# Modulation ahead of h: three of eight k-blocks of the adaLN product go from VectorE to TensorE

## The chip, the cores and the metric

The kernel runs on one core of one Trainium2 chip. The metric is the device time of one execution in microseconds (us), and lower is better. The engines are called as in the profile: PE is TensorE (PEld is its weight loads), DVE is VectorE, ACT is ScalarE, POOL is GpSimd, SP is SyncE, which issues the DMAs here.

## The reference, cut to what matters

One layer of a decoder trunk reads a normalized input `h` that is modulated by a vector `c`. Everything behind it (two token mixers, their merge, an output projection and a last norm) starts from `h`:

```python
ada = jax.nn.silu(c) @ w_ada + b_ada
shift, scale, gate = jnp.split(ada, 3, axis=-1)
h = _rmsnorm(x, norm_w) * (1.0 + scale[:, None, :]) + shift[:, None, :]
proj = jnp.einsum("bsd,de->bse", h, w_in)
...
```

`x` is 1024 tokens by 1024 channels in float32, `c` is one row of 1024, `w_ada` is 1024 by 3072, and `w_in` is 1024 by 8472. The change concerns the first line alone, for `shift` and `scale`: a product of one row by a matrix.

## The kernel before

All channels are cut into eight blocks of 128, numbered by `k` where they are the channels of `h`. The front of the kernel, its first 80 us or so, does the following.

SP loads `x` in eight tiles `xt` (128 tokens each), the part of `w_ada` for shift and scale in eight tiles `wa` of 1 MB (one for each `k`, five buffers), and the first weights of `w_in` (`wr`). Each `xt` is squared and summed on ACT (L259), its factor is made on POOL (`rs`, L262), and DVE scales it in place (L263).

`ada_cols(k)` makes shift and scale for the 128 channels of block `k`. Tile `was[k]` holds, on 128 partitions, eight k-blocks of the sum over the input channels, each with 256 columns (128 for scale, 128 for shift). DVE multiplies each of the eight blocks with its column of `cols` (silu of `c`) and adds them up in `acc`, 128x256: one instruction at L287 and seven at L289. What is left is the sum over the 128 partitions, and TensorE does it with two matmuls (L291) whose weights are the halves of `acc` and whose moving operand is a single column of ones. They write two columns of the bank `cp`, of which there is one buffer. DVE reads them into the columns `av` (L294) and `sv` (L296).

`h_half(k, hf)` makes block `k` of `h` for one half of the tokens. TensorE transposes four pieces of `xt` into the bank `tp` (L302), ACT applies `av` and `sv` (`xa`, L305) and rounds to the high part `hh` (L306), and DVE subtracts to get the low part `hl` (L307). Float32 products are made from three matmuls on high and low parts.

`c_half` (L115 to L117) multiplies: for three slabs of `w_in` at a time (`FIRST`), nine matmuls with 512 moving columns for each block `k` and token half, accumulated over all `k` in the banks `mm` (first half) and `um` (second half). So these products follow `h` block by block.

Behind the front, DVE and POOL form sums of the blocks of `h` (`pe`, L440 to L444) for a product scheme with fewer multiplications, and TensorE goes on with the other projections.

The order of the instructions on each engine isn't that of the code. A scheduler in the compiler sorts the whole program along a timeline of its own before it is built, and each engine then works through its list strictly in that order.

Of the kernel before, what the change touches and what calls it, by code (L numbers as in the profile page):

```python
# [31 lines left out]
P = 128  # L32
# [32 lines left out]
PAIRS += [(G0 + 12, G0 + 13), (G0 + 14, G0 + 15)]  # L65
R_C, R_SHIFT, R_SCALE, R_NW, R_SNW, R_BG, R_CB, R_CW = 0, 8, 16, 24, 32, 40, 56, 66
NROWS = 106


def build(ctx, tc, t):  # L70
    nc = tc.nc
    V, A, G, PE, SP = nc.vector, nc.scalar, nc.gpsimd, nc.tensor, nc.sync
# [75 lines left out]
    ones = const.tile([P, P], F32, name="ones")  # L148
# [5 lines left out]
    V.memset(mhalf, -0.5)  # L154
    cols = const.tile([P, NROWS], F32, name="cols")
    hb = const.tile([P, 40], F32, name="hb")
# [45 lines left out]
    with tc.tile_pool(name="st", bufs=1, side="right") as st, \  # L202
            tc.tile_pool(name="stp", bufs=1, space=PSUM) as stp:
        vrow = st.tile([NROWS, P], F32, name="vrow")
        SP.dma_start(out=vrow, in_=t["vecs"])
        xts, was, uraw = {}, {}, {}
# [31 lines left out]
        vps = stp.tile([P, 512], F32, tag="tp", bufs=1, name="tp")  # L238
        PE.transpose(out=vps[:, :NROWS], in_=vrow, identity=ident[:NROWS, :NROWS])
        V.tensor_copy(out=cols, in_=vps[:, :NROWS])  # L240
        V.tensor_scalar(out=cols[:, R_CB:NROWS], in0=cols[:, R_CB:NROWS], scalar1=0.5, scalar2=None, op0=ALU.mult)
        V.tensor_scalar(out=cols[:, R_BG:R_BG + 16], in0=cols[:, R_BG:R_BG + 16], scalar1=0.5, scalar2=None,
# [37 lines left out]
        def ada_cols(k):  # L280

            cp = stp.tile([P, 512], F32, tag="cp", bufs=1, name="cp")
            acc = st.tile([P, 256], F32, tag="acc", bufs=2, name="acc")
            for kk in range(8):
                w = was[k][:, kk, :]
                if kk == 0:
                    V.tensor_scalar(out=acc, in0=w, scalar1=cols[:, kk:kk + 1], scalar2=None, op0=ALU.mult)  # L287
                else:
                    V.scalar_tensor_tensor(out=acc, in0=w, scalar=cols[:, kk:kk + 1], in1=acc, op0=ALU.mult, op1=ALU.add)  # L289
            for i in range(2):  # L290
                PE.matmul(cp[:, 2 * i:2 * i + 1], lhsT=acc[:, i * P:(i + 1) * P], rhs=ones[:, 0:1],  # L291
                          start=True, stop=True)
            a, sh = av[:, k:k + 1], sv[:, k:k + 1]
            V.scalar_tensor_tensor(out=a, in0=cp[:, 0:1], scalar=cols[:, R_SCALE + k:R_SCALE + k + 1],  # L294
                                   in1=cols[:, R_NW + k:R_NW + k + 1], op0=ALU.add, op1=ALU.mult)
            V.tensor_tensor(out=sh, in0=cp[:, 2:3], in1=cols[:, R_SHIFT + k:R_SHIFT + k + 1], op=ALU.add)  # L296
# [12 lines left out]
        for k in range(2):  # L309
            ada_cols(k)  # L310
            h_half(k, 0)
        for k in range(2):
            h_half(k, 1)
        for k in range(2, 8):
            ada_cols(k)
            for hf in range(2):
                h_half(k, hf)
# [312 lines left out]
    with tc.tile_pool(name="sd", bufs=1, side="right") as sd, \  # L630
# [152 lines left out]
        for tb in range(8):  # L783
            PE.matmul(rps[:, 2 * tb:2 * tb + 1], lhsT=sacc[:, tb * P:(tb + 1) * P], rhs=ones[:, 0:1],
                      start=True, stop=True)
# [455 lines left out]
```

## Time and profile before

| | |
|---|---|
| median of 3 runs | 1285.14 us (1281.14 to 1290.57) |
| the profiled execution | 1286.09 us, of which the span of its instructions is 1284.4 us |
| busy share of the span | PE 92%, PEld 77%, DVE 75%, POOL 60%, ACT 46% |
| mean granted clock of TensorE | 0.974 |

A busy share is an average over the whole span. The front has other limits than the rest, so the views below are cut to stretches of it.

### The profile page before, as it was taken

What the parts mean: (1) busy time and instruction counts of PE and PEld (TensorE: products, weight loads), DVE (VectorE), ACT (ScalarE), POOL (GpSimd) and SP (SyncE); (2) the same over time, 40 slices, a digit from 0 to 9 for tenths busy, and PEclk for the clock granted to TensorE, in tenths of its full rate; (3) what the DMA queues carried; (4) which work ended last, traced back from release to release, by engine and by line L of the source; (5) the groups of instructions that cost most, each with busy time, mean ns of one, the idle gap of its engine ahead of it and who ended that gap; (6) DMA issues with size and microseconds to landing.
All of it is one profiled execution on the core that took longest, in us unless ns stands there. A gap on an engine that the chain in (4) does not pass through costs nothing. (4 is left out here: it accounts for less than half of the span.)

```text
span 1284.4 us, 18783 instructions
## 1 busy us (share of the span) xinstructions
PE 1183.9 (92%) x6206; PEld 988.8 (77%) x6206; DVE 963.1 (75%) x1618; ACT 594.8 (46%) x1194; POOL 776.1 (60%) x644
## 2 busy tenths in 40 slices
PE   4897899999978999999988999999999999999896
PEld 3686688777766788799778888888887787878685
DVE  6979767787799566348689764545667968999997
ACT  5443324242423232477667733444456553444354
POOL 3258465474755476448887966435446635587666
PEclk9998899998989999999999999999999999999999
DMA  8422443624556566654565558623236619766143
GB/s 346 158 100 98 160 123 124 213 64 167 188 185 216 175 211 228 223 177 148 188 200 163 173 191 296 210 87 116 74 127 210 201 55 328 224 188 193 52 116 145
DMA packets 104126, 219.70 MB, mean 171 GB/s; under 512 B 11818, under 2 KB 19420, under 8 KB 103004
## 3 DMA queue, kind: packets, MB, share of 16 engines
q1 hardware_dynamic: 104028, 218.50, 51.5%
q8 instruction: 49, 0.80, 0.3%
q14 instruction: 49, 0.40, 0.1%
HBM read 154.85 MB, written 63.61 MB: 170 GB/s over the span
## 5 line engine op out<-in xcount | busy, mean ns | idle before, releaser
L103 POOL TENSOR_TENSOR wl<-wr,wh 128x512 fp32r<-128x512 f32 (+1 forms) x188 | 281.5, 1508 | 135.7 <-ACT wh L102 130.7
L102 ACT CAST wh<-wr 128x512 fp32r<-128x512 f32 (+1 forms) x214 | 129.8, 618 | 158.4 <-DMA wr<-w_c 53.7
L103 POOL TENSOR_TENSOR sl<-sr,sh 128x512 fp32r<-128x512 f32 x57 | 91.0, 1603 | 78.8 <-ACT sh L102 65.7
L115 PE MATMUL mm<-hh,wh 128*128 128x512 f32 x288 | 115.9, 407 | 4.3 <-ACT wh L102 1.9
L116 PE MATMUL mm<-hl,wh 128*128 128x512 f32 x288 | 116.7, 405 | 3.0 <-DVE hl L307 3.0
L117 PE MATMUL mm<-hh,wl 128*128 128x512 f32 x288 | 116.3, 405 | 0.0
L102 ACT CAST sh<-sr 128x512 fp32r<-128x512 f32 x57 | 34.1, 619 | 96.6 <-DVE sr L478 77.0
L140 PE MATMUL mm<-wh,hh 128*128 128x256 f32 (+1 forms) x256 | 74.9, 294 | 3.8 <-DVE tmp L348 3.8
L141 PE MATMUL mm<-wl,hh 128*128 128x256 f32 (+1 forms) x256 | 74.8, 293 | 0.0
L142 PE MATMUL mm<-wh,hl 128*128 128x256 f32 (+1 forms) x256 | 74.4, 292 | 0.0
L1018 ACT ACTIVATE pr<-pr,sm 128x1024 f32<-128x1024 f32 (+3 forms) x64 | 49.9, 780 | 50.4 <-DVE sm L1017 42.4
L1021 POOL TENSOR_SCALAR pr<-pr,sm 128x1024 f32<-128x1024 f32 (+3 forms) x64 | 48.6, 762 | 34.7 <-DVE sm L1020 30.2
L1013 DVE CUSTOM_DVE_ANT_0 pr<-lg,fb 128x512 f32<-128x512 f32 (+1 forms) x96 | 51.5, 551 | 23.5 <-PE lg L1012 14.0
L115 PEld LDWEIGHTS mm<-hh,wh 128*128 128x128 f32 x288 | 55.1, 193 | 15.6 <-ACT wh L102 2.4
L116 PEld LDWEIGHTS mm<-hl,wh 128*128 128x128 f32 x288 | 55.3, 192 | 14.7 <-DVE hl L307 3.9
L1004 POOL TENSOR_SCALAR_AFFINE_SELECT fb<-fb 128x128 f32<-128x128 f32 x64 | 21.9, 344 | 72.1 <-DVE sm L1013 57.3
L117 PEld LDWEIGHTS mm<-hh,wl 128*128 128x128 f32 x288 | 55.2, 192 | 10.8
L1037 DVE TENSOR_TENSOR ptl<-tp,pth 128x512 fp32r<-128x512 f32 (+1 forms) x80 | 50.1, 632 | 15.9 <-ACT pth L1036 15.5
L1036 ACT CAST pth<-tp 128x512 fp32r<-128x512 f32 (+1 forms) x80 | 42.3, 543 | 41.5 <-PE tp L1033 32.4
L683 ACT ACTIVATE ab<-ab,acs 128x128 f32<-128x128 f32 x128 | 41.1, 391 | 31.7 <-DMA ab<-a_scr 28.1
L140 PEld LDWEIGHTS mm<-wh,hh 128*128 128x128 f32 x256 | 49.5, 194 | 4.7 <-DVE tmp L348 4.5
L103 POOL TENSOR_TENSOR m<-ab,m 128x512 fp32r<-128x512 f32 x32 | 46.7, 1462 | 7.1 <-ACT m L102 4.7
(393 smaller groups left out, 3972.6 us busy)
## 6 DMA issues: line engine op xcount, KB each, us to landing
wr<-w_c SPq DMA_DIRECT2D x116, 256.0 KB, 3.5
wa<-w_ada SPq DMA_DIRECT2D x8, 1024.0 KB, 11.4
g_scr<-gt SPq DMA_DIRECT2D x16, 512.0 KB, 4.0
ab<-a_scr SPq DMA_DIRECT2D x32, 256.0 KB, 3.7
gt<-g_scr SPq DMA_DIRECT2D x32, 256.0 KB, 3.0
wr<-w_ps SPq DMA_DIRECT2D x28, 256.0 KB, 2.9
wr<-w_pa SPq DMA_DIRECT2D x28, 256.0 KB, 3.1
wr<-so SPq DMA_DIRECT2D x28, 256.0 KB, 2.6
```

The source lines that it names most:

```text
L102: A.copy(out=hi[:, :n], in_=raw[:, :n])
L103: eng.tensor_tensor(out=lo[:, :n], in0=raw[:, :n], in1=f32(hi[:, :n]), op=ALU.subtract)
L115: PE.matmul(ps, lhsT=hi[:, cs], rhs=xh[k][:, hs], start=(k == 0), stop=False)
L116: PE.matmul(ps, lhsT=hi[:, cs], rhs=xl[k][:, hs], start=False, stop=False)
L117: PE.matmul(ps, lhsT=lo[:, cs], rhs=xh[k][:, hs], start=False, stop=(k == 7))
L140: PE.matmul(o, lhsT=xh[k][:, ts], rhs=hi[:, cs], start=(k == 0), stop=False)
L141: PE.matmul(o, lhsT=xh[k][:, ts], rhs=lo[:, cs], start=False, stop=False)
L142: PE.matmul(o, lhsT=xl[k][:, ts], rhs=hi[:, cs], start=False, stop=(k == 7))
L1013: V.tensor_tensor_reduce(out=pr[:, n0:n1], in0=lg[:, :n1 - n0], in1=fb[:, n0:n1], op0=ALU.add, op1=ALU.min, scale=1.0, scalar=BIG, accum_o ...
L1018: A.activation(out=pr[:, :n], in_=pr[:, :n], func=AF.Exp, scale=-1.0, bias=sm[:, 0:1], accum_out=sm[:, 1:2])
L1021: G.tensor_scalar(out=pr[:, :n], in0=pr[:, :n], scalar1=sm[:, 1:2], scalar2=0.5, op0=ALU.mult, op1=ALU.mult)
L1037: V.tensor_tensor(out=ptl[:, :w], in0=tp[:, :w], in1=f32(pth[:, :w]), op=ALU.subtract)
```

## The change

A constant `NV = 5` is added. DVE sums up the first five k-blocks only. The other three go to TensorE as matmuls of their own, with a 128x128 piece of `was[k]` as weights and the column of `cols` as the moving operand, into the same column of `cp` into which the sum of `acc` then goes, with `acc` last. The type of all of them is float32, as it was for `acc`.

```diff
+NV = 5
...
-            for kk in range(8):
+            for kk in range(NV):
                 w = was[k][:, kk, :]
...
             for i in range(2):
-                PE.matmul(cp[:, 2 * i:2 * i + 1], lhsT=acc[:, i * P:(i + 1) * P], rhs=ones[:, 0:1],
-                          start=True, stop=True)
+                o = cp[:, 2 * i:2 * i + 1]
+                for kk in range(NV, 8):
+                    PE.matmul(o, lhsT=was[k][:, kk, i * P:(i + 1) * P], rhs=cols[:, kk:kk + 1], start=(kk == NV),
+                              stop=False)
+                PE.matmul(o, lhsT=acc[:, i * P:(i + 1) * P], rhs=ones[:, 0:1], start=False, stop=True)
```

For all eight `k` together these are 24 instructions less on DVE (three of the seven at L289, eight times) and 48 matmuls more on TensorE (three for each of two columns, eight times). Four lines are added in the code, so L291 becomes L296 (the new matmuls are L294), L302 becomes L306, and c_half's L115 to L117 become L116 to L118.

The scheduler makes another order of it within the front. From DVE's last `hl` on, the instructions of all five engines stand in the same order as before.

On TensorE, around the products of block `k` = 3 (`hh_234` and `hl_242`; `hh_235` is block 4), before:

```order
L291 MATMUL cp<-ones,acc 128x1 x2
L116 MATMUL um<-hl_242,wh 128x512
L117 MATMUL um<-hh_234,wl 128x512
L116 MATMUL um<-hl_242,wh 128x512
L117 MATMUL um<-hh_234,wl 128x512
L116 MATMUL um<-hl_242,e_379 128x512
L117 MATMUL um<-hh_234,e_379 128x512
L291 MATMUL cp<-ones,acc 128x1 x2
L302 MATMUL tp<-ident,xt 128x128 x4
L115 MATMUL mm<-hh_235,wh 128x512 x2
```

and the same place after:

```order
L118 MATMUL um<-hh_234,e_379 128x512
L294 MATMUL cp<-cols,wa 128x1 x3
L296 MATMUL cp<-ones,acc 128x1
L294 MATMUL cp<-cols,wa 128x1 x3
L306 MATMUL tp<-ident,xt 128x128 x4
L296 MATMUL cp<-ones,acc 128x1
L116 MATMUL mm<-hh_235,wh 128x512
L117 MATMUL mm<-hl_243,wh 128x512
L118 MATMUL mm<-hh_235,wl 128x512
```

Eight one-column matmuls of one `k` now stand between two groups of nine c_half matmuls, where two stood. The group shown of after is that of `k` = 7, the last one. The two shown of before are those of `k` = 4 and 5; those of `k` = 6 and 7 came later, one behind each half of the products of block 5.

On VectorE, from the start of the sum for `k` = 4 (DVE's row L287) on, before:

```order
L287 TENSOR_SCALAR acc<-wa,cols 128x256
L289 SCALAR_TENSOR_TENSOR acc<-wa,cols,acc 128x256 x4
L307 TENSOR_TENSOR hl_241<-xa,hh_233 128x512
L289 SCALAR_TENSOR_TENSOR acc<-wa,cols,acc 128x256
L294 SCALAR_TENSOR_TENSOR av<-cp,cols 128x1
L296 TENSOR_TENSOR sv<-cp,cols 128x1
L287 TENSOR_SCALAR acc<-wa,cols 128x256
L289 SCALAR_TENSOR_TENSOR acc<-wa,cols,acc 128x256 x2
L307 TENSOR_TENSOR hl_241<-xa,hh_233 128x512
L289 SCALAR_TENSOR_TENSOR acc<-wa,cols,acc 128x256 x3
L307 TENSOR_TENSOR hl_242<-xa,hh_234 128x512
L289 SCALAR_TENSOR_TENSOR acc<-wa,cols,acc 128x256 x3
```

and after:

```order
L288 TENSOR_SCALAR acc<-wa,cols 128x256
L290 SCALAR_TENSOR_TENSOR acc<-wa,cols,acc 128x256 x4
L311 TENSOR_TENSOR hl_241<-xa,hh_233 128x512
L298 SCALAR_TENSOR_TENSOR av<-cp,cols 128x1
L300 TENSOR_TENSOR sv<-cp,cols 128x1
L288 TENSOR_SCALAR acc<-wa,cols 128x256
L290 SCALAR_TENSOR_TENSOR acc<-wa,cols,acc 128x256 x3
L311 TENSOR_TENSOR hl_241<-xa,hh_233 128x512
L290 SCALAR_TENSOR_TENSOR acc<-wa,cols,acc 128x256
L298 SCALAR_TENSOR_TENSOR av<-cp,cols 128x1
L300 TENSOR_TENSOR sv<-cp,cols 128x1
```

Fewer instructions of the sums now stand between the rows that others wait for (`hl`, `av`, `sv`); the last sum is finished in the order ahead of the `hl` of block 4, where before it ran on until behind that of block 5.

## Rows read from the trace of the kernel before

**Rows 1.** Windows: length; busy us of PE, PEld, DVE, ACT, POOL; PEclk; DMA; GB/s.
```profile
31.30:40.00 8.70, 7.30 (x40) 5.55 (x39) 8.65 (x22) 3.48 (x6) 1.58 (x1) 1.00 0.95 389
40.00:50.00 10.00, 9.05 (x47) 7.34 (x47) 9.96 (x18) 5.03 (x9) 4.73 (x3) 1.00 0.47 145
50.00:60.50 10.50, 7.69 (x32) 5.81 (x32) 10.36 (x23) 5.20 (x8) 2.96 (x2) 0.84 0.18 50
60.50:72.60 12.10, 12.10 (x66) 10.19 (x65) 4.04 (x11) 5.59 (x8) 0.00 (x0) 1.00 0.01 2
sum 41.30, PE 36.14 PEld 28.89 DVE 33.01 ACT 19.30 POOL 9.27; mean PE 9.04 PEld 7.22 DVE 8.25 ACT 4.82 POOL 2.32
```
**Rows 2.** TensorE's longest waits, 31.3 to 72.6 us: us, times, longest.
```profile
PE mm L116 <- DVE hl L307: 2.3, 1, 2.3
PE um L116 <- DVE hl L307: 1.3, 2, 0.9
```
**Rows 3.** Timeline of TensorE: start, us, engine, line, operation, tiles, shape.
```profile
53.67 0.60 PE L302 MATMUL tp<-ident,xt 128*128 128x128 f32 x4
56.58 0.50 PE L116 MATMUL mm<-hl,wh 128*128 128x512 f32 x1 [2.31 <-DVE hl L307]
...
57.55 0.63 PE L117 MATMUL mm<-hh,wl 128*128 128x512 f32 x1
57.98 0.63 PE L116 MATMUL mm<-hl,e 128*128 128x512 f32 x1
```
**Rows 4.** Windows around the same place, columns as in group 1.
```profile
51.20:53.90 2.70, 2.20 (x15) 1.67 (x14) 2.63 (x2) 2.67 (x5) 2.70 (x2) 1.00 0.19 22
53.90:56.60 2.70, 0.39 (x5) 0.15 (x3) 2.70 (x9) 1.64 (x3) 0.10 (x1) 1.00 0.53 172
57.15:60.56 3.41, 3.41 (x11) 2.63 (x10) 3.38 (x8) 0.00 (x0) 0.00 (x0) 0.50 0.00 0
```
**Rows 5.** Groups by line, VectorE, 29.2 to 64 us: busy us, mean ns, idle before.
```profile
L289 DVE SCALAR_TENSOR_TENSOR acc<-wa,cols,acc 128x256 f32<-128x256 f32 x42 | 25.0, 627 | 0.3
```
**Rows 6.** Timeline of TensorE and of its weight loads, 64.0 to 65.1 us.
```profile
64.25 0.50 PE L291 MATMUL cp<-ones,acc 128*128 128x1 f32 x4
64.62 0.63 PE L302 MATMUL tp<-ident,xt 128*128 128x128 f32 x4
65.00 0.48 PE L115 MATMUL um<-hh,wh 128*128 128x512 f32 x1
...
64.03 0.64 PEld L291 LDWEIGHTS cp<-ones,acc 128*128 128x128 f32 x4
64.51 0.51 PEld L302 LDWEIGHTS tp<-ident,xt 128*128 128x128 f32 x4
64.98 0.30 PEld L115 LDWEIGHTS um<-hh,wh 128*128 128x128 f32 x2
```
**Rows 7.** L291's weight loads in the whole trace: min/median/max ns.
```profile
L291 PEld LDWEIGHTS cp<-ones,acc x32: 186/192/337, 11.6 to 67.4; 128*128 128x128 f32 x32
```
**Rows 8.** Timeline of VectorE without and with POOL's work beside it.
```profile
33.39 2.45 DVE L289 SCALAR_TENSOR_TENSOR acc<-wa,cols,acc 128x256 f32<-128x256 f32 x6
...
51.03 2.96 POOL L103 TENSOR_TENSOR wl<-wr,wh 128x560 fp32r<-128x560 f32 x2 [3.41 <-ACT wh L102]
51.23 3.05 DVE L289 SCALAR_TENSOR_TENSOR acc<-wa,cols,acc 128x256 f32<-128x256 f32 x2
```
**Rows 9.** Timeline of the front's end on TensorE and VectorE.
```profile
72.64 0.60 PE L302 MATMUL tp<-ident,xt 128*128 128x128 f32 x4
...
74.74 0.69 DVE L307 TENSOR_TENSOR hl<-xa,hh 128x512 fp32r<-128x512 f32 x1 [1.83 <-ACT hh L306]
75.54 2.39 DVE L440 TENSOR_TENSOR pe<-hh,hl 128x512 f32<-128x512 f32 x2
```
**Rows 10.** Windows behind the front, columns as in group 1.
```profile
90.00:100.00 10.00, 6.89 (x52) 6.43 (x50) 9.96 (x9) 3.02 (x6) 8.16 (x6) 1.00 0.66 224
150.00:160.00 10.00, 10.00 (x45) 8.12 (x44) 4.46 (x9) 3.79 (x6) 5.47 (x5) 1.00 0.77 288
```

## The prediction

> **What bounds the kernel now.** The chain that ended last covers only the tail of the program, so it says nothing of the front. I read the windows of the front first, then TensorE's waits in it, then single rows. The reader is to see that the front changes its bound. From 31.3 to 60.5 us VectorE works without a break (8.65 of 8.70 us, 9.96 of 10.00, 10.36 of 10.50), while TensorE has holes; from 60.5 us on TensorE is busy for 12.10 of 12.10 us, and VectorE mostly waits [rows 1]. VectorE's load is the sum in acc: 42 instructions of L289 take 25.0 us of the stretch from 29.2 to 64 us [rows 5]. TensorE's longest waits are for hl, which stands behind those sums in VectorE's queue [rows 2]. So VectorE delays TensorE until about 60 us, and TensorE works off the rest by itself. What matters for the end is the last hl: VectorE starts the next stage 0.1 us after it [rows 9], is then busy nearly all the time, and from 150 us on TensorE is at 10.00 of 10 us [rows 10]. The order behind the front is unchanged, so I expect a shift of the last hl to reach the end in full, whichever way it goes.
>
> **Step 1: what VectorE gets rid of.** 24 instructions of L289 go, 18 of them for k = 2 to 7, in the stretch that counts. Back to back one takes 2.45/6 = 0.41 us; held up beside POOL it takes 3.05/2 = 1.5 us [rows 8], and the mean is 0.63 [rows 5]. 18 x 0.41 = 7.4 us at least, 18 x 0.63 = 11.3 us at the mean. With that the last sum ends some 7 to 11 us earlier and VectorE is no longer what TensorE waits for. This is no gain by itself: it is worth what TensorE makes of it.
>
> **Step 2: what TensorE can win back.** I follow TensorE from the transposes at 31.3 us to those at 72.64 us, from which the last hl comes 2.1 us later [rows 9]. In these 41.3 us it is busy for 36.14 us, so 5.2 us are idle [rows 1]. A stop costs a little more than the idle time shown, as the modelled ends overlap the next start in a stream: four transposes take 0.38 us in a stream (64.62 to 65.00) [rows 6], so those at 53.67 were over at 54.05 in that sense, and the hole to 56.58 is 2.53 us and not 2.31 [rows 3]. There are six such stops, 0.2 us each, 1.2 us. Last, right behind the longest hole (0.39 of 2.70 us busy) the granted clock is 0.50, TensorE's lower level of 1.2 GHz, for 3.41 us [rows 4], and products of 512 columns follow each other at 0.43 us [rows 3]. That loses 3.41 x 0.5 = 1.7 us. If the holes go, this low stretch should go with them. Together 5.2 + 1.2 + 1.7 = 8.1 us, and not more can be won here, however early VectorE is.
>
> **Step 3: what TensorE gets to do.** For k = 2 to 7 there are 6 x 6 = 36 new matmuls. A float32 matmul of this kind leaves two records (the two of L291 show as x4), each with its own load of 128 weight columns, so 72 records. Their form is that of L291 and has its price in the trace. Four records of L291 take 0.37 us from 64.25 to the next start at 64.62, 0.093 each; their weight loads, which pace such a run, start 0.48 us ahead of the next four, 0.12 each [rows 6]. A weight load all by itself has a median of 192 ns [rows 7]. Now six, two and six stand in a row where four stood, so less of the loading hides behind a long product. I take 0.11, between the two paces of rows 6: 72 x 0.11 = 7.9 us. The ends are 72 x 0.093 = 6.7 and 72 x 0.19 = 13.7 us. All of it lies on TensorE's own path: from about 32 us on it would have no wait left in which to hide.
>
> **Step 4: what goes at nothing.** For k = 0 and 1 the same is done ahead of 31.3 us. The loads of x and of the first wa tiles pace that part (the DMA share is still 0.95 up to 40 us [rows 1]), VectorE has six instructions less there and TensorE twelve matmuls more, which partly fill its waits. I put it at 0, with 1 us either way. The later wa tiles don't hold up the new matmuls, although these read wa themselves and free its buffers later: the DMA share is 0.18 from 50 us on, and the first use of the last tile on TensorE stands behind the products of block 3. The new matmuls bring one new wait: cp has one buffer, so the first of them for the next k waits until VectorE has read av and sv, and the products of block k-1 or k-2 queue behind it. In the new order VectorE has only two to four sums ahead of av, some 0.8 to 1.6 us, while TensorE has nine products (2.1 us) to do, so I take that as covered.
>
> **Sum.** -8.1 + 7.9 = -0.2 us. The profiled execution of 1286.1 us would become 1285.9. It was 1 us above the median of the runs, 1285.1, so against the median I say 1285 us: no change. The work is moved from an engine that had no time to one that had just enough.
>
> **Rivals.** First, a gain: the new matmuls cost TensorE little, because their weights load while a product of 512 columns is still running, as the first load of L291 does (it starts at 64.03, 0.2 us ahead of its matmul) [rows 6]. At half the lowest pace, 0.047, the 72 records take 3.4 us, the sum is -4.7 and the time 1280.4 us. Against it: in the order six of them follow each other, and only the first has such a cover. The Trainium skill, page "TensorE: Matmul & The Clock Gate", section "Back-to-back issue gap", puts a matmul of 1 to 64 columns at about 60 cycles, 25 ns; by that the new ones would take an estimated 72 x 0.025 = 1.8 us, the sum would be -6.3 us, and the time 1278.8. The trace's 0.093 for four records with their weights speaks against that, and agrees with what the same page's section on LDWEIGHTS says, that 128 columns of weights take 128/1.2 = 107 ns. Chance 0.12.
>
> Second, slower, by the clock. TensorE's granted clock fell after the one stretch in which it did little [rows 4]. In the new order, from the products of block 1 to those of block 3, every 2.1 us of products alternates with sixteen one-column records and four transposes, 20 x 0.11 = 2.2 us in which few columns move. If that is too little, the clock falls more often. Each low stretch like that of rows 4 costs 1.7 us; the one of before is already counted as won back, so from the second on the change is slower by this alone. For it: the stretch of thin work is new, about 22 us long. Against it: from 51.2 to 53.9 us TensorE did much the same (one group of L291, eight transposes, three products) and the clock stayed at 1.00 [rows 4]. Three low stretches give -0.2 + 5.1 = +4.9 us, 1290 us; the whole 22 us at half clock gives 11 us, 1296. Chance 0.25.
>
> Third, the new wait is not covered: VectorE is held up beside POOL (1.5 us for one instruction of L289 in place of 0.41 [rows 8]) just when TensorE's queue stands at cp. Three such cases at 1 us each give 1288 us. Chance 0.08.
>
> **How the numbers follow.** The forecast has 0.55, from 1283 to 1288 us. The lower end of the range takes in most of the first rival, 1279.5; the upper end the second with three low stretches and the price of lone weight loads (13.7 - 8.1 = +5.6, 1290.7), so 1291.5. What is left out on both sides is about 0.15 to 0.2, also because single runs of before lie between 1281 and 1291. A change of 1%, 12.9 us, is about what a measurement of this kernel can tell from no change. The most that can be won is 8.1 us, so faster by over 1% has 0.02, for something that I don't see. Slower by over 1% needs the low clock all through and more: 0.03. The rest, 0.95, is within 1%.
>
> **What would show it.** In the profile of the changed kernel VectorE should have clear idle time from about 50 us on, and TensorE none from about 32 us to the last hl, with the granted clock at 1.00 from there to 75 us. The new L294 records should come at 0.09 to 0.12 us each in a row (step 3). The last hl should start within 2 us of 74.7 us, and the rest should follow shifted by as much. It is wrong if TensorE still waits for hl or acc for microseconds (step 1), if the records cost 0.05 or 0.19 us (step 3), if the clock falls in the stretch of thin work, or if the end moves by another amount than the last hl.

## The result, and the profile after

The changed kernel takes 1289.76 us (median of 20 runs, 1285.88 to 1294.27), the kernel before 1287.32 us in the same series (20 runs). The ratio is 1.0026, with a 95% interval from 1.0014 to 1.0038: 1.8 to 4.9 us slower. In 1285.14 us, the median that the prediction starts from, that is some 1288.5 us. The range held it, and it is far inside 1%; but the forecast said that nothing would move, and something small did, to the slower side. The profiled execution took 1293.57 us (span 1291.8 us).

These are the windows of the front in the changed kernel (length; busy us of PE, PEld, DVE, ACT, POOL; PEclk; DMA; GB/s), to be laid beside [rows 1]:

```profile
20.00:31.30 11.30, 8.74 (x30) 6.72 (x29) 8.60 (x19) 6.86 (x12) 4.30 (x7) 1.00 0.83 331
31.30:40.00 8.70, 8.70 (x46) 7.28 (x45) 7.02 (x15) 4.04 (x7) 2.85 (x3) 1.00 0.89 344
40.00:50.00 10.00, 10.00 (x73) 9.22 (x73) 8.91 (x19) 3.37 (x5) 2.08 (x2) 1.00 0.47 184
50.00:60.50 10.50, 10.50 (x71) 9.45 (x70) 4.33 (x14) 5.32 (x8) 2.73 (x2) 1.00 0.11 27
60.50:72.60 12.10, 12.10 (x65) 9.97 (x64) 3.39 (x5) 6.37 (x9) 0.00 (x0) 1.00 0.07 22
```

TensorE is busy in every microsecond from 31.3 us on. VectorE, which had 10.36 of 10.50 us to do from 50 us on, has 4.33. No stretch of low clock is recorded. Up to here it is the picture that the prediction drew. (Below, a record is one matmul as the profile lists it, of which a float32 matmul leaves two; "thin" is a matmul with one moving column, a product is one with 512, and the stream is TensorE's work from the four transposes ahead of block 1's second half to the last four transposes of the front.) One period of the new stream on TensorE (timeline; start, us, engine, line, operation):

```profile
52.31 0.40 PE L118 MATMUL mm<-hh,e 128*128 128x512 f32 x1
52.55 0.72 PE L294 MATMUL cp<-cols,wa 128*128 128x1 f32 x6
53.13 0.36 PE L296 MATMUL cp<-ones,acc 128*128 128x1 f32 x2
53.36 0.81 PE L294 MATMUL cp<-cols,wa 128*128 128x1 f32 x6
54.03 0.63 PE L306 MATMUL tp<-ident,xt 128*128 128x128 f32 x4
54.50 0.28 PE L296 MATMUL cp<-ones,acc 128*128 128x1 f32 x2
54.64 0.71 PE L116 MATMUL um<-hh,wh 128*128 128x512 f32 x2
```

The sixteen records of one column start at 52.55, and the products go on at 54.64; less the four transposes (0.38 us in a stream, [rows 6]) that is 1.71 us, 0.107 us for each record.

What the windows hide stands at the left edge, in the timeline of TensorE ahead of the transposes for the second half of block 1 (33.61):

```profile
25.18 0.96 PE L306 MATMUL tp<-ident,xt 128*128 128x128 f32 x3 [0.36 <-ACT xa L309]
28.12 0.48 PE L306 MATMUL tp<-ident,xt 128*128 128x128 f32 x1 [1.99 <-DVE xt L264]
28.39 1.28 PE L294 MATMUL cp<-cols,wa 128*128 128x1 f32 x6
29.53 1.20 PE L116 MATMUL mm<-hh,wh 128*128 128x512 f32 x2
30.53 0.63 PE L118 MATMUL mm<-hh,e 128*128 128x512 f32 x1
...
32.67 0.63 PE L118 MATMUL mm<-hh,wl 128*128 128x512 f32 x1
33.09 0.45 PE L117 MATMUL mm<-hl,e 128*128 128x512 f32 x1
33.38 0.39 PE L118 MATMUL mm<-hh,e 128*128 128x512 f32 x1
33.61 0.60 PE L306 MATMUL tp<-ident,xt 128*128 128x128 f32 x4
```

The new matmuls of k = 2 stand in a row of six records at 28.39 and take 1.14 us, 0.19 each, because the clock is still at its lower level: the products behind them follow at 0.43 us, and only from 33.1 us on at 0.23 to 0.29. (PEclk shows 1.00 here all the same: the record of the clock has no entry before its first rise, at 33.2 us. In such a stretch the pitch of the products tells, 0.43 us at the lower level and 0.23 at the upper.) The transposes at 33.61 are the ones that the prediction had at 31.3. From them to the last transposes, at 73.72, it is 40.1 us where it was 41.36. So the front ends like this (timeline; compare [rows 9]):

```profile
73.72 0.60 PE L306 MATMUL tp<-ident,xt 128*128 128x128 f32 x4
...
75.82 0.69 DVE L311 TENSOR_TENSOR hl<-xa,hh 128x512 fp32r<-128x512 f32 x1 [1.83 <-ACT hh L310]
76.61 2.39 DVE L444 TENSOR_TENSOR pe<-hh,hl 128x512 f32<-128x512 f32 x2
```

So the start is 2.3 us later, the stream 1.25 us shorter, and the end of the front 1.08 us later.

### The profile page after: what moved, and what is told of

Same layout as the page of the kernel before. It is cut to its first block, busy times and chain, and to the rows that moved or that the text cites. A ratio compares the mean times of both kernels' runs of the same rounds, so it can differ in the third digit from the quotient of the medians.

```text
span 1291.8 us, 18958 instructions
## 1 busy us (share of the span) xinstructions
PE 1198.1 (93%) x6302; PEld 1004.6 (78%) x6302; DVE 956.2 (74%) x1594; ACT 595.5 (46%) x1194; POOL 771.3 (60%) x644
## 5 line engine op out<-in xcount | busy, mean ns | idle before, releaser
L116 PE MATMUL mm<-hh,wh 128*128 128x512 f32 x288 | 116.5, 409 | 3.9 <-ACT wh L103 1.9
L117 PE MATMUL mm<-hl,wh 128*128 128x512 f32 x288 | 116.6, 405 | 0.0
L118 PE MATMUL mm<-hh,wl 128*128 128x512 f32 x288 | 116.5, 406 | 0.0
L116 PEld LDWEIGHTS mm<-hh,wh 128*128 128x128 f32 x288 | 55.0, 193 | 14.7 <-ACT wh L103 2.4
L117 PEld LDWEIGHTS mm<-hl,wh 128*128 128x128 f32 x288 | 55.5, 193 | 11.0
L118 PEld LDWEIGHTS mm<-hh,wl 128*128 128x128 f32 x288 | 55.4, 192 | 11.1
L1040 ACT CAST pth<-tp 128x512 fp32r<-128x512 f32 (+1 forms) x80 | 42.4, 543 | 42.6 <-PE tp L1037 33.5
L687 ACT ACTIVATE ab<-ab,acs 128x128 f32<-128x128 f32 x128 | 41.1, 391 | 33.1 <-DMA ab<-a_scr 33.0
L143 PEld LDWEIGHTS mm<-wh,hl 128*128 128x128 f32 x256 | 50.4, 197 | 0.0
```

What stands on the lines that cost most here:

```text
L116: PE.matmul(ps, lhsT=hi[:, cs], rhs=xh[k][:, hs], start=(k == 0), stop=False)
L117: PE.matmul(ps, lhsT=hi[:, cs], rhs=xl[k][:, hs], start=False, stop=False)
L118: PE.matmul(ps, lhsT=lo[:, cs], rhs=xh[k][:, hs], start=False, stop=(k == 7))
L143: PE.matmul(o, lhsT=xl[k][:, ts], rhs=hi[:, cs], start=False, stop=(k == 7))
```

## The experiments

There are two theories. **A**: the time follows the end of the front, and the change loses in its early part, ahead of 33 us, more than it wins behind. **B**: something behind the front costs a few microseconds more. At the end a table puts all whole kernels side by side. Times are medians; the kernel before took 1287.15 to 1287.59 us in the same series.

**The change once more** (no edit).

> The changed kernel once more, as a control. Both theories expect the same front: last hl at 75.8 us, 1.1 us later than before. Theory A (the front alone: the end moves by what the last hl moves, and the 7.4 us between the two profiled executions are mostly spread of single executions): the time is 0.1% above before, about 1 us, and a second profile shows shifts behind the front that differ from those of the first by several us. Theory B (something behind the front costs 2 to 6 us more, in the same place each time): 0.25 to 0.5% above before, and the second profile shows the shift growing by over 1 us again at the same places, 415, 640 to 700 and 1110 to 1170 us.

1290.83 us (12 runs), ratio 1.0030 [1.0015, 1.0044]. The loss is real, and by the time alone it has the size that B gave; the 1 us of A lies outside the interval. But the places that B named are not the change's own. From 640 to 700 us VectorE's distance to the first profile of before grows by 2.8 us in the change's first profile and by 0.2 in its second, and it grows by 1.8 in the second profile of the kernel before (below); from 1110 to 1170 us these are 1.7, 0.3 and 1.7. The first two windows are of this profile; the third is from the cut changed kernel below:

```profile
24.10:34.40 10.30, 7.62 (x24) 5.57 (x23) 8.82 (x19) 3.53 (x6) 3.78 (x4) 0.50 0.80 319
34.40:72.60 38.20, 38.20 (x239) 33.59 (x238) 20.36 (x46) 18.20 (x28) 6.65 (x5) 1.00 0.30 108
```
```profile
25.10:35.30 10.20, 7.95 (x25) 6.40 (x26) 9.19 (x17) 3.04 (x7) 3.23 (x3) 0.50 0.94 372
```

Here the low stretch is recorded: the granted clock is 0.50 to 34.4 and to 35.3 us. In both the clock had risen once before, at 20.7 and 21.7 us, and it fell again at 24.1 and 25.1, behind a wait for e (1.24 us, to 23.70, in the first of them). The last hl starts at 76.39 and 76.87 us, later than in the first profile.

**A pure delay.** In the kernel before, the last four transposes are issued four times, so that only the end of the front moves.

```
-            for i in range(4):
+            for i in (0, 1, 2, 3) * (4 if (k, hf) == (7, 1) else 1):
```

> The kernel before with nothing moved, but the last four transposes of the front issued four times over: a pure delay of 12 x 0.11 = 1.3 us on TensorE ahead of the last hl, with the order behind it unchanged. Last hl at 76.0 us. Theory A: the time is 1.3 us (0.1%) above before. Theory B in the form that a shift of the front against the rest is what costs: 3 us or more (0.25%) above before, as the change. If the change costs 3 us and this shift 1, the cost behind the front belongs to the change itself and not to its delay.

1287.13 us (0.9988 [0.9972, 1.0003]), no loss, although the last hl starts at 77.05 us in its profile. Part of that shift is chance: the low stretch behind the long wait at 54 us lasted 6.8 us here and 3.4 in the profile of before. Still, by A alone +1.3 us and more were due, and that lies outside the interval, which ends at +0.4. This speaks against A at this size, and it stays unexplained.

**VectorE's part alone.** VectorE sums five of eight blocks and TensorE none, so three eighths of the sum for shift and scale are left out.

```
-                for kk in range(NV, 8):
-                    PE.matmul(o, lhsT=was[k][:, kk, i * P:(i + 1) * P], rhs=cols[:, kk:kk + 1], start=(kk == NV),
-                              stop=False)
-                PE.matmul(o, lhsT=acc[:, i * P:(i + 1) * P], rhs=ones[:, 0:1], start=False, stop=True)
+                PE.matmul(o, lhsT=acc[:, i * P:(i + 1) * P], rhs=ones[:, 0:1], start=True, stop=True)
```

> VectorE's part alone: it sums up five of the eight k-blocks, and TensorE doesn't do the other three, so three eighths of shift and scale are left out. Theory A with the ledger of step 2: TensorE's stops and the low stretch of the clock go and nothing comes in their place; last hl at 68 to 69 us, 6 to 7 us earlier than before, time 6 to 7 us below before. The rival (VectorE wasn't what TensorE waited for, the loads were): last hl within 2 us of before.

1282.52 us (0.9951 [0.9929, 0.9973]), -6.3 us; the last hl starts at 69.24 us, 5.5 earlier, a little less than A said. The stream starts 0.8 us earlier (30.52) and is 4.7 us shorter (36.6 in place of 41.4); 2.2 us of waits for hl are still left in it (the view of TensorE's waits, from 31 us on). The gain reaches the end of the program.

**Six blocks on VectorE** in place of five (NV = 6).

> Two of eight k-blocks on TensorE in place of three (six stay on VectorE). By the ledger TensorE gets 48 records for k = 2 to 7 in place of 72, so 2.6 us less at 0.11 us each, while VectorE, which in the changed kernel was idle for 6 of the 10.5 us from 50 to 60.5 us, still is early enough: last hl at 72.5 to 73.5 us, 1 to 2 us earlier than before, and the time 1 to 2 us below before by theory A. If instead the stops come back (VectorE the bound again), last hl at 75 us or later. Theory B expects the time 1 to 4 us above what the last hl says.

1288.31 us (1.0009 [0.9991, 1.0026]); the last hl at 75.29 us, where 72.5 to 73.5 was expected. The clock was at 0.50 twice in the front (windows, columns as above). The second stretch, inside the stream, costs half of its 3.4 us, which is nearly all of the miss:

```profile
25.30:32.10 6.80, 5.79 (x17) 4.83 (x18) 5.80 (x10) 3.10 (x7) 2.54 (x4) 0.50 0.67 262
42.40:45.80 3.40, 3.40 (x11) 2.83 (x12) 3.26 (x10) 0.00 (x0) 0.00 (x0) 0.50 0.32 97
```

**Late part and early part of the change.** NV is 8 for k = 0 to 2 and 5 from k = 3 on, or the other way round. (Here and below, a tile with all eight blocks on VectorE starts its bank with the matmul of acc.)

```
-NV = 5
+NVS = (8, 8, 8, 5, 5, 5, 5, 5)
...
+            NV = NVS[k]
```

> VectorE keeps all eight k-blocks for the first three tiles of wa (k = 0, 1, 2), as in the kernel before; from k = 3 on three blocks go to TensorE, as in the change. Ledger of the front (A): the loss of the change lies in its early part, where the first thin matmuls stand ahead of block 1's products and the clock rises late. Without them TensorE's four transposes ahead of block 1's second half should start at 31.3 to 32.0 us (before and the shifted copy), not at 33.6, the stream from there should take some 40 us as in the change, and the last hl start at 73.5 to 74.5 us; the time is then 1 us below that of before to equal with it (1286 to 1288, ratio 0.999 to 1.000), 2 to 4 us below the change's. Something behind the front (B, the time does not follow the last hl): as slow as the change, ratio 1.002 to 1.003, whatever the last hl shows. Third: if the late start comes from the transfers or from chance and not from the thin matmuls, the start stays at 33 us or more and the last hl at 75.5 or later.

1287.16 us (0.9997 [0.9979, 1.0016]). The transposes that start the stream come at 31.54 us, the last hl at 73.97: both as A said. Without the early part of the change, its order and its thin matmuls, the late start is gone.

> The other part alone: three blocks on TensorE for k = 0, 1, 2, all eight on VectorE from k = 3 on. Ledger of the front (A): the start at 33 to 34 us and a rise of the clock at 33 us or later, as in the change; behind it only the waits for VectorE's sums, less the 4 to 6 us that VectorE is ahead by nine sums fewer; the last hl at 75 to 76.5 us, the time 1288 to 1291, ratio 1.001 to 1.003. If the rise of the clock does not depend on the thin matmuls, the start is 31.5 us and the last hl 73 us, ratio 0.998 to 0.999. B: between before and the change, 1.001.

1286.26 us (0.9980 [0.9966, 0.9995]), faster than both kernels. The start is late, 33.75 us, as A said, but the last hl starts at 72.74 us, not at 75 to 76.5: I had priced what nine sums less on VectorE give at too little. Behind the start TensorE waits 2.0 us in all (1.2 for hl, 0.8 for acc), there is no low stretch in the middle, and six records of new thin matmuls are left to pay for in place of 66.

**The kernel before once more** (no edit, one profiled execution).

> The kernel before once more, for its front alone. If its profiled front is typical, TensorE's clock rises at 29.8 us, falls for some 3.4 us behind the longest hole at 53 to 57 us, and the last hl starts at 74.7 us within 0.5. If the low stretch is not in every execution, the last hl starts 1.7 us earlier, at about 73, and the change's last hl (75.8 and 76.4 in its two profiles) is then 3 us later than the usual one of before, which is what the times differ by.

Its last hl starts at 74.53 us, with the same low stretch at 57 us, so [rows 9] are no exception. Its start is not that of the first profile (timeline of TensorE):

```profile
31.88 0.63 PE L117 MATMUL mm<-hh,e 128*128 128x512 f32 x1
32.31 0.85 PE L302 MATMUL tp<-ident,xt 128*128 128x128 f32 x4
```

The clock rose at 32.8 us, not at 29.8, and the transposes came 1.0 us later; and yet the front ended 0.2 us earlier, because TensorE's waits took up the delay: the long one for hl is 2.3 us in both, but all waits from 31 us on together are 5.0 us in the first profile and 3.9 in this one. The two executions have spans of 1284.4 and 1289.4 us with fronts that end alike. So what two profiles differ by late in the program is not evidence.

**Four kernels cut behind the second pair of slabs**, so that everything behind some 160 us is left out: before, the change, the delay, and the early part.

```
-        for n, (sa, sb) in enumerate(PAIRS):
+        for n, (sa, sb) in enumerate(PAIRS[:2]):
...
+    for k in range(8):
+        SP.dma_start(out=t["out"][k * P:(k + 1) * P, :], in_=g_scr[4 + k % 2])
+    hctx.close()
+    return
```

> The kernel before, cut behind the second pair of slabs (some 160 us of its span; a copy of two stored slabs to the output ends it), so all later stages are left out. It is the base for the three other cut kernels: its own time says nothing, its profile should show the front of the whole kernel, the last hl at 74.5 to 74.8 us with one low stretch of the clock at 57 us. Its runs should lie much closer together than those of the whole kernel (within 2 us in place of 9), since fewer stretches of the clock can fall out one way or the other.

> The changed kernel with the same cut. If the whole cost of the change lies in the front, its median is above that of the cut kernel before by what the last hl is later: 1.1 to 1.7 us by the two profiles of the change (A). If the profiles caught early fronts and most executions have a later one, the difference is 3 to 4 us, that of the whole kernels. If it is 1 us or less while the whole kernels differ by 3.4 and 3.9, the remaining 2 us come behind 160 us (B).

> The kernel before with the last four transposes issued four times, same cut. The twelve transposes more are 1.3 us by 0.11 each; its whole version showed the last hl 2.3 us later in the profile, but no loss in the time (-1.5 us, interval -3.6 to +0.4). A: above the cut kernel before by 1.3 to 2.3 us. If a later front is made up for within the next 80 us, it is 0 to 0.5 us.

> Three blocks on TensorE for k = 0, 1, 2 alone, same cut. Its whole version had the last hl at 72.7 us and was 2.6 us faster (0.6 to 4.4). A: 2 us below the cut kernel before (1.5 to 2.5), the full front's gain. If the gain of the whole version was chance, 0 to 1 us.

| cut kernel | median us (runs) | lowest to highest | last hl in its profile |
|---|---|---|---|
| before | 193.17 (4) | 191.84 to 193.79 | 75.82 |
| the change | 195.28 (4) | 192.98 to 195.71 | 76.87 |
| the delay | 193.16 (4) | 192.87 to 194.56 | 75.50 |
| early part | 190.69 (5) | 190.37 to 191.85 | 73.20 |

By the medians the change loses 2.1 us, the early part gains 2.5, and the delay of 1.3 us can't be seen. With four runs on a side the 2.1 is not clear of chance: one of the changed kernel's runs, 192.98 us, lies below the median of before (its granted clock was 0.924, in the other three 0.908 to 0.909, in the four of before 0.921 to 0.925). It also lies between the 1.1 to 1.7 us that A said and the 3 to 4 us of the other case. The expected front of the cut kernel before was missed by 1 us: its low stretch in the middle lasted 6.8 us, and 3.4 in the whole kernel's two profiles and in that of the cut delay. That alone is 1.7 us, enough for the delay's front to end earlier here. Behind the front the two profiles keep a distance of 1.05 us, to 140 us; then the changed one has a low stretch at 144.6 us which the other hasn't (windows of the cut kernel before, then of the cut change), and the distance is 2.15. All four profiles of the whole kernels, two of before and two of the change, have such a stretch at 142 to 147 us, so this half of the 2.1 us looks like chance and not like a cost of the change:

```profile
140.00:152.00 12.00, 9.47 (x44) 7.11 (x43) 8.42 (x23) 3.98 (x8) 4.63 (x4) 1.00 0.05 14
```
```profile
140.00:152.00 12.00, 9.81 (x40) 7.21 (x39) 8.74 (x22) 2.66 (x6) 4.79 (x4) 0.86 0.05 14
```

**What delays the rise of the clock.** Three blocks on TensorE for two tiles alone, or for three.

```
-NV = 5
+NVS = (8,8,8,5,5,8,8,8)
```

```
-NV = 5
+NVS = (8,8,5,5,5,8,8,8)
```

> Three blocks on TensorE for k = 3 and 4 alone, all eight on VectorE elsewhere: the start of the front keeps the order of before, VectorE is relieved by six sums (2.5 to 3.8 us) where TensorE waits for it, TensorE gets 24 records (2.6 us). A: the transposes ahead of block 1's second half start at 31.3 to 32.3 us as in the five fronts with the order of before; TensorE's idle time behind it falls from 5 us to 1 to 3 us; the last hl starts at 71 to 73 us, the time is 2 to 3.5 us below before, ratio 0.997 to 0.9985. If VectorE's relief is lost to other waits or a low stretch of the clock stays behind 53 us, the last hl is at 73.5 to 74.5 us and the ratio 0.999 to 1.000.

> The same for k = 2, 3 and 4: three thin matmuls now stand in TensorE's queue between the products of block 1, as one single edit of the early part. If the late start in the change comes from its reordering for k = 0 and 1 (all four transposes of a half ahead of the products, two of the products of block 0 ahead of the wait only), the start is still 31.5 to 32.5 us and the last hl at 70.5 to 72.5 us. If thin matmuls at the lower clock are enough for it, the start is 33 us or more and the last hl 0.5 us or more later than with two tiles. Ratio 0.996 to 0.998 and 0.998 to 1.000.

Two tiles: 1286.86 us (0.9997 [0.9982, 1.0012]), last hl at 72.53 us: the front ended where A said, but the gain of 2 us and more in the time that A expected with it was not seen. Three tiles: 1287.53 us (0.9999 [0.9982, 1.0016]), last hl at 76.23 us. Both kernels have the order of before for k = 0 and 1. The timeline of TensorE with two tiles:

```profile
27.45 1.05 PE L116 MATMUL mm<-hh,wh 128*128 128x512 f32 x2
28.63 0.48 PE L307 MATMUL tp<-ident,xt 128*128 128x128 f32 x1
...
32.32 0.83 PE L307 MATMUL tp<-ident,xt 128*128 128x128 f32 x4
32.90 0.70 PE L116 MATMUL um<-hh,wh 128*128 128x512 f32 x2
33.44 0.39 PE L116 MATMUL um<-hh,e 128*128 128x512 f32 x1
33.67 0.39 PE L117 MATMUL um<-hl,wh 128*128 128x512 f32 x1
```

and with three:

```profile
28.16 1.27 PE L295 MATMUL cp<-cols,wa 128*128 128x1 f32 x6
...
32.96 1.06 PE L307 MATMUL tp<-ident,xt 128*128 128x128 f32 x4
33.81 0.43 PE L297 MATMUL cp<-ones,acc 128*128 128x1 f32 x2
34.09 1.42 PE L295 MATMUL cp<-cols,wa 128*128 128x1 f32 x6
35.38 0.56 PE L297 MATMUL cp<-ones,acc 128*128 128x1 f32 x2
35.80 1.20 PE L116 MATMUL um<-hh,wh 128*128 128x512 f32 x2
36.80 0.63 PE L117 MATMUL um<-hl,wh 128*128 128x512 f32 x1
37.23 0.63 PE L118 MATMUL um<-hh,wl 128*128 128x512 f32 x1
```

With two tiles the clock rises at 32.8 us: products at 0.23 us from 33.4 on. With three, twelve thin records of wa stand ahead of and behind block 1's products, and the products still follow at 0.43 us until the clock rises at 42.0 us, although TensorE never stops (window of the same kernel):

```profile
31.30:42.00 10.70, 10.70 (x37) 8.94 (x35) 7.06 (x17) 2.98 (x6) 1.57 (x1) 1.00 0.92 363
```

One tile more on TensorE moves the last hl by 3.7 us to the wrong side. The start, 32.96 us, fell into the gap between the two answers of the expectation; the rise of the clock decides. In the times the two kernels differ by 0.7 us only, so either the late rise isn't in most executions, or 3.7 us at the front's end don't show in the time; one profile of each can't tell.

**All whole kernels.** Start of the stream, rise of the clock and last hl are from one profile each; the last two columns are the distance to the kernel before, from [rows 9] and from the ratio. In the change again, VectorE's part alone and six on VectorE the clock had been up once before, from 20.7, 21.7 and 21.9 us on; the rise listed is the second one.

| kernel | start | rise | last hl | last hl, distance | time, distance (95%) |
|---|---|---|---|---|---|
| before | 31.28 | 29.8 | 74.74 | 0 | 0 |
| before again | 32.31 | 32.8 | 74.53 | -0.2 | |
| the change | 33.61 | 33.2 | 75.82 | +1.1 | +3.4 (+1.8 to +4.9) |
| the change again | 34.05 | 34.4 | 76.39 | +1.65 | +3.9 (+1.9 to +5.7) |
| pure delay | 32.02 | 31.7 | 77.05 | +2.3 | -1.5 (-3.6 to +0.4) |
| VectorE's part alone | 30.52 | 28.5 | 69.24 | -5.5 | -6.3 (-9.1 to -3.5) |
| six on VectorE | 32.42 | 32.1 | 75.29 | +0.55 | +1.2 (-1.2 to +3.3) |
| late part | 31.54 | 30.5 | 73.97 | -0.8 | -0.4 (-2.7 to +2.1) |
| early part | 33.75 | 33.3 | 72.74 | -2.0 | -2.6 (-4.4 to -0.6) |
| two tiles | 32.32 | 32.8 | 72.53 | -2.2 | -0.4 (-2.3 to +1.5) |
| three tiles | 32.96 | 42.0 | 76.23 | +1.5 | -0.1 (-2.3 to +2.1) |

The nine timed rows lie within -3.8 to +2.3 us of what their front's end says, and on the mean within 0.1 us. So there is no sign of a cost behind the front that all of them share, and a single comparison is good to 2 to 4 us. More than that the table doesn't show. The kernel with VectorE's part alone carries most of the agreement; among the other eight rows, front ends from -2.2 to +2.3 us go with times from -2.6 to +3.9 without a clear order. And both rows of the change miss to the same side, by 2.3 us.

How far a shift of the front is passed on can be read from the profiles themselves. The same instruction of VectorE, some 60 instructions behind the last hl, in the profiles of before, of the change and of the delay (timeline):

```profile
134.70 0.68 DVE L478 TENSOR_TENSOR sr<-sr,wr 128x512 f32<-128x512 f32 x1
```
```profile
135.76 0.68 DVE L482 TENSOR_TENSOR sr<-sr,wr 128x512 f32<-128x512 f32 x1
```
```profile
137.16 0.68 DVE L478 TENSOR_TENSOR sr<-sr,wr 128x512 f32<-128x512 f32 x1
```

The change is 1.06 us behind there, 1.08 at the last hl; the delay 2.46, and 2.31 at the last hl. In the eight profiles of the other rows the distance there is within 0.1 us of the one at the last hl. So the shift is passed on in full for the next 60 us; from 142 us on a low stretch that comes or doesn't, and then many places further behind, move the executions against each other by microseconds.

## Why the prediction was right or wrong

**What bounds.** Right. VectorE is free from 50 us on, TensorE has no wait from 31 us on, and a shift of the last hl is passed on in full to 140 us. That it reaches the end of the program in full, as the prediction said, is not shown: the gain of VectorE's part alone does, the pure delay doesn't.

**Step 1** (VectorE loses 18 sums): right. 24 instructions of L290 are left, the last of which starts at 53.2 us, where there were 42 and the last started at 63.0. That is 9.8 us earlier, within the 7 to 11 of the forecast.

**Step 2** (TensorE can win back 8.1 us): right in kind, the holes and the low stretch at 57 us are gone. VectorE's part alone made the stream 4.7 us shorter with 2.2 us of waits left, 6.9 us of the 8.1 together.

**Step 3** (0.11 us a record): right, 0.107 us. 66 of the 72 records lie behind the start, 7.1 us. With step 2 the stream should have become 1.0 us shorter and became 1.25 us shorter in the first profile. The first rival fell with this: the Trainium skill's 25 ns for a matmul of few columns (page "TensorE: Matmul & The Clock Gate", section "Back-to-back issue gap") is the gap of an isolated matmul by that section's own words, and not what a row of float32 matmuls with a load of weights each costs here. By the same page of the Trainium skill, section "LDWEIGHTS (loading the stationary operand)", a load takes its number of columns over 1.2 in ns, an estimate of 107 ns for 128. The row's 0.107 us agrees; the 0.093 of rows 6, for which the prediction said the same, is 13% below.

**Step 4 failed**: "For k = 0 and 1 the same is done ahead of 31.3 us. [...] I put it at 0, with 1 us either way." The start of the stream came at 33.61, 34.05 and 34.12 us in three profiles of the change, against 31.28, 32.31, 32.11, 32.02 and 32.02 in five that have the order of before: 2.0 us later on the mean. The sum with these numbers is -1.25 for the stream and about +2 for the start, so a later end of the front, where it had 0 for the start and -0.2 in all.

Three things make up the late start. All four transposes now stand ahead of the products, and the fourth waits 1.99 us for xt, while two products that used to run ahead of it (27.61 us) stand behind it. Then come six thin records of k = 2 at the low clock, 1.14 us. And in part of the executions the clock rises later: at 33.2 to 35.3 us, against 29.8 to 32.8. The first two can be told from the third in a pair in which the clock stays low up to the start in both, the second profile of before and then the second of the change (timeline of TensorE):

```profile
28.62 0.48 PE L302 MATMUL tp<-ident,xt 128*128 128x128 f32 x1
28.75 0.78 PE L117 MATMUL mm<-hh,e 128*128 128x512 f32 x1
```
```profile
28.23 0.47 PE L306 MATMUL tp<-ident,xt 128*128 128x128 f32 x1 [1.99 <-DVE xt L264]
28.50 1.28 PE L294 MATMUL cp<-cols,wa 128*128 128x1 f32 x6
29.64 1.20 PE L116 MATMUL mm<-hh,wh 128*128 128x512 f32 x2
34.05 0.75 PE L306 MATMUL tp<-ident,xt 128*128 128x128 f32 x4
```

The fourth transpose is done 0.25 us earlier in the change, the thin records take 1.14 us (28.50 to 29.64), and then ten products follow in 4.41 us where eight took 3.56 (28.75 to 32.31). -0.25 + 1.14 + 0.85 = 1.74 us, the whole distance of the two starts. So the order and the thin records make 1.7 us by themselves; between the first profiles (2.3 us) the same sum is 1.45, as the fourth transpose is 0.54 us earlier there, and the clock, up at 29.8 us in one and at 33.2 in the other, makes the other 0.9. That thin matmuls can hold the rise back much longer is suggested by two tiles against three, one execution of each.

A second slip stands behind it: I took TensorE's start as a thing that would show in the end either way. In the kernel before it doesn't, as its second profile shows (1 us later, the same end), since TensorE has waits to take it up. The change removes just these waits, so a late start has nothing left that takes it up. In the early part alone, which starts as late (33.75 us) and saves the later thin matmuls, the front ends earlier all the same.

**The rivals.** The second, slower by the clock, had the mechanism but not the place: it looked at the thin work behind 36 us, where the clock stayed at 1.00 in all profiles of the change. Only with six blocks on VectorE did it fall there (42.4 us). The third, the wait for cp, didn't occur.

**What stays open.** The front's end is later by 1.1 and 1.65 us in the change's two full profiles, the times by 3.4 and 3.9. So less than half of the measured loss is accounted for by the front as profiled. The rest, about 2 us, is of the size by which other rows miss to either side, and one stretch of low clock more or less, as at 144.6 us, makes 1.1 us; but it is there in both series of the change, so its cause is open and not shown to be chance. One lead is the clock: the mean granted clock is 0.974 in the 20 runs of the change and 0.973 in its 12 more, against 0.976 in 30 runs of before. How much of that is the front itself, these means don't tell. The delay that cost nothing (-1.5 us where +1.3 were due) isn't explained either.

## What to carry to other kernels

Work that moves from the engine that is waited for to the one that waits fills the holes, and these holes were also what took up a late start; price the start of the stretch as carefully as its length, by the order on the engine and not by the transfers alone. Moving the three blocks for the first three of the eight tiles alone (0.9980 [0.9966, 0.9995]) was better here than moving them for all eight: VectorE gets ahead early, and TensorE keeps some wait. It is the best of several variants, so the 0.2% may be partly luck, but its cut form was faster as well. And one profile of each kernel doesn't settle a microsecond: the front of the kernel before ended between 74.5 and 75.8 us (its cut form included), two executions of it with equal fronts had spans 5 us apart, and the cut kernels' times had a third of the spread (1.5 to 2.7 us in place of 6 to 11).

## What the runs showed of the hardware

That the clock can stay low while TensorE never stops: 10.70 of 10.70 us busy, in a mix of thin matmuls, transposes and products, and products at 0.43 us up to 42.0 us, in one execution. That a rise need not last: in the change's second profile the clock was up from 20.7 us and fell at 24.1 us, behind a wait of 1.24 us. The thin matmuls at full clock didn't make it fall in the change's later stream, with sixteen records and four transposes between every nine products. And the same low stretch had another length in another execution of the same code (3.4 and 6.8 us at 56 us, in the kernel before and its cut form as with the delay), so that two executions differ by 1.7 us in this one place.
